# An MLP block in two phases of seven block products: hidden features stored in DRAM, w_out applied by Strassen's scheme

## The chip, the cores and the metric

The kernel runs on one core of one Trainium2 chip. The metric is the device time of one execution in microseconds (us). Engines are named as in the profile: PE does the matmuls, DVE and ACT work elementwise, POOL and SP mostly issue DMAs.

## The reference

One layer of a diffusion transformer, for 2048 tokens of width 1024 with an inner width of 4096, all in fp32:

```python
h = h + gate1 * rmsnorm(short_gated_conv(modulate(rmsnorm(h, g_pre), shift1, scale1)), g_post)
f = square(relu(modulate(rmsnorm(h, g_pre_ff), shift2, scale2) @ w_in)) @ w_out     # 1024 -> 4096 -> 1024
h = h + gate2 * rmsnorm(f, g_post_ff)
```

Shifts, scales and gates come from silu(c) @ ada_w + ada_b. The change is in the second line and in the norm behind it.

## The kernel before

Everything is held transposed: features on the 128 partitions, tokens along the free axis, in NB = 4 token blocks of TB = 512. An fp32 product is made of three fp32r matmuls: each operand is split into a high part (a cast on ACT, L113) and a low part (a subtraction on DVE, L114), and high·high, high·low and low·high are added up in a PSUM bank (`mm3`, `project`, L132). One matmul has a 128x128 weight tile and 512 token columns.

The program has two parts. The conv part runs over the four token blocks and takes about the first third of the span (`conv_in`, `conv_out`); at its end each block's residual stream is stored to DRAM (`hbuf`). The MLP part runs over pairs of token blocks p = (0, 1), (2, 3), and for each pair over NCH = 8 chunks of FC = 512 inner features. In a chunk, `mlp_in` makes the hidden features of both blocks (tile names `hid`, then `r` after the relu, `s` after the square, `hh` as the split pair), and `mlp_out` multiplies them by the chunk's part of w_out (`f`). Each of the 8 x 2 output tiles of a chunk is a PSUM bank of its own that takes 12 matmuls; it is then added by DVE to a running sum in SBUF (`accumulate`, L335; in chunk 0 ACT copies it instead, L333). The six banks of the pool `acc` go round, so a bank that has been filled is not needed again until five others have been filled. Hidden features stay in SBUF.

The last chunk of the last pair is written out by hand (`mlp_last`): the output of the last block is made in two halves of 256 tokens, so that the norm and the residual of the first half (`finish_shared`, shared out over DVE, POOL and ACT) run while PE works on the second half.

The order on each engine is set by a scheduler at build time, which lists every engine's instructions; at run time each engine takes its list in order and waits on semaphores. Weight loads and stores are issued by SP in such an order, too.

Of the kernel before, what the change touches and what calls it, by code (L numbers as in the profile page):

```python
# [9 lines left out]
F32 = mybir.dt.float32  # L10
F32R = mybir.dt.float32r
# [3 lines left out]
P = 128  # L15
# [6 lines left out]
FC = 512  # L22
NCH = DFF // FC
FB = FC // P
EPS = 1e-6


@with_exitstack
def conv_block_kernel(ctx: ExitStack, tc: tile.TileContext, xt, c, cols, ada, w_first, w_sci, w_sco, w_in, w_out,
# [62 lines left out]
    silu = y_pair("silu").rearrange("p s n -> p (s n)")  # L92
# [23 lines left out]
    def load_weights(src, name, n=D, eng=nc.vector):  # L116
        raw = sbuf([P, D], F32, "wraw", 4, f"{name}_raw")
        nc.sync.dma_start(raw[:, :n], src)
        hi = sbuf([P, D], F32R, "whi", 3, f"{name}_hi")
        lo = sbuf([P, D], F32R, "wlo", 3, f"{name}_lo")  # L120
        split(hi[:, :n], lo[:, :n], raw[:, :n], eng)
        return hi, lo
# [17 lines left out]
    class RootMean:  # L140
# [21 lines left out]
        def rows(self):  # L162
            name, n = self.name, self.n
            ps = tp_bank(f"{name}_ps")[:, :n]
            hi, lo = stat_tile(f"{name}_hi", F32R)[:, :n], stat_tile(f"{name}_lo", F32R)[:, :n]
# [11 lines left out]
        def rows_of(self, ps):  # L177
# [6 lines left out]
            r = row_tile(f"{name}_r")[:, :n]  # L184
# [8 lines left out]
    def shifted(v, k, sh, name):  # L193

        hi, lo = act_tile(f"{name}_hi"), act_tile(f"{name}_lo")
# [13 lines left out]
    def mod_tile(j):  # L209

        for m in range(2):
            mod_sum(m, j, sbuf([P, D], F32, "gh", 8, f"ada{j}_{m}"))
# [4 lines left out]
    def mod_rest(m):  # L217

        for j in range(KT):
            mod_sum(m, j, sbuf([P, D], F32, "wraw", 4, f"adar{m}_{j}"))  # L220
            yield
# [14 lines left out]
    def gate_split(q, j):  # L236
        gh, gl = act_tile(f"gh{q}_{j}"), act_tile(f"gl{q}_{j}")
# [3 lines left out]
    def gate(q, j, pc, pv, pb):  # L241
# [29 lines left out]
        if j % 2 == 0:  # L271
            pair = gh_tile(f"g{q}_{j}", F32)
            gated[q, j], gated[q, j + 1] = pair[:, 0], pair[:, 1]
# [14 lines left out]
    def conv_out(q):  # L288
# [11 lines left out]
        for i in range(KT // 2):  # L300
            xr = load_pair(xt[q, i], f"xr{q}_{i}")
# [5 lines left out]
            nc.gpsimd.dma_start(hbuf[q][i], xr)  # L307
        nc.gpsimd.dma_start(rbuf[q], ssh.rows())


    def mlp_in(ch, a, between=None):

        hid = {q: [] for q in a}
        for f in range(FB):
            w = load_weights(w_in[ch * FB + f], f"wi{min(a)}_{ch}_{f}")
            for q in a:
                name = f"{q}_{ch}_{f}"
                ps = acc_bank(f"hid{name}")
                project(w, a[q], ps)
                r = tmp_tile(f"r{name}")  # L320
                nc.scalar.activation(r, ps, AF.Relu)  # L321
                s = tmp_tile(f"s{name}")
                nc.vector.tensor_mul(s, r, r)  # L323
                h = gh_tile(f"hh{name}")
                split(h[:, 0], h[:, 1], s)
                hid[q].append((h[:, 0], h[:, 1]))
            if f == 0 and between:
                between()
        return hid

    def accumulate(y, ps, ch, ss):
        if ch == 0:
            nc.scalar.copy(y, ps)  # L333
        else:
            nc.vector.tensor_add(y, ps, y)  # L335
        if ch == NCH - 1:
            ss.add(y)

    def mlp_out(ch, hid, y, ss):
        for i in range(KT // 2):  # L340
            w = load_weights(w_out[i, ch], f"wf{min(hid)}_{ch}_{i}")
            for s in range(2):
                j = 2 * i + s
                ws = [t[:, s * FC:(s + 1) * FC] for t in w]
                for q in hid:
                    ps = acc_bank(f"f{q}_{ch}_{j}")
                    project(ws, hid[q], ps)
                    accumulate(y[q][j], ps, ch, ss[q])

    def mlp_finish(q, y, r):  # L350
        for i in range(KT // 2):
            hr = load_pair(hbuf[q][i], f"hr{q}_{i}")
            for s in range(2):
# [214 lines left out]
```

## Time and profile before

| what | value |
|---|---|
| median of 3 runs | 2150.74 us (2150.71 to 2150.82) |
| the profiled execution | 2149.79 us, its span 2148.0 us |
| PE busy | 2117.8 us, 99% of the span, 9366 matmuls |
| DVE, ACT, POOL busy | 52%, 31%, 3% |
| DMA | 226.47 MB, mean 105 GB/s |

The profiled execution's own time is 1.79 us above its span. Busy shares are of the span. A matmul's listed length contains the overlap with its neighbours; what one costs in a stream is read from the chain of waits, where a run of matmuls has its start, length and count.

### The profile page before, as it was taken

The numbers are of one execution on the slowest core, as the hardware profiler recorded it, in microseconds if no ns is written. First come the engines' busy times: TensorE is split into PE (matmuls) and PEld (weight loads), VectorE is DVE, ScalarE is ACT, GpSimd is POOL, SyncE is SP. The second block draws the span as 40 slices with busy tenths as digits, with TensorE's granted clock in tenths as the row PEclk, the third lists the DMA queues.
The fourth block names the chain that finished last, engine by engine and source line by source line (L and its number), as shares of the span: only waits on it lengthen the run. The fifth ranks groups of instructions, "written<-read, shape, count | busy, mean of one in ns | idle before, by whom it ended". The sixth has DMA issues, their size and how long they took to land.

```text
span 2148.0 us, 23105 instructions
## 1 busy us (share of the span) xinstructions
PE 2117.8 (99%) x9366; PEld 1749.1 (81%) x9366; DVE 1113.8 (52%) x1626; ACT 655.8 (31%) x940; POOL 69.2 (3%) x72
## 2 busy tenths in 40 slices
PE   7999999999999999999999999999999999999997
PEld 4788888888888888888888888888888888888886
DVE  8877766664655862333333333496233333333356
ACT  3342244433325543121121221353212112121152
POOL 2000000000000000000000000000000000000006
PEclk8999999999999999999999999999999999999998
DMA  8665533432533441111111111136111111111113
GB/s 323 227 225 205 177 138 141 168 134 92 200 139 128 181 172 48 45 46 49 49 49 49 50 49 49 63 124 235 49 49 45 46 49 49 49 49 50 49 59 118
DMA packets 65514, 226.47 MB, mean 105 GB/s; under 512 B 7424, under 2 KB 9472, under 8 KB 65408
## 3 DMA queue, kind: packets, MB, share of 16 engines
q1 hardware_dynamic: 61056, 210.84, 27.9%
q0 software_dynamic: 3776, 13.63, 1.7%
q8 instruction: 73, 1.20, 0.2%
q10 hardware_dynamic: 576, 0.52, 0.1%
q14 instruction: 33, 0.27, 0.0%
HBM read 207.15 MB, written 17.83 MB: 105 GB/s over the span
## 4 chain that ended last, share of the span: by engine, by line
PE 96%; DVE 3%; ACT 0%; issue 0%; DMA 0%; SPq 0%; DVEq 0%
PE hid L132 32%; PE f L132 32%; PE c L132 23%; PE y_ps L132 8%; DVE ada L207 1%; PE c L475 0%; DVE rf_sq L160 0%; DVE a_lo L197 0%; DMA xt<-in_xt_dram 0%; DVE mods L215 0%; DVE a_v L191 0%; DVE f L372 0%; DVE f L335 0%; DVE hr L375 0%; DVE rx_sq L157 0%
## 5 line engine op out<-in xcount | busy, mean ns | idle before, releaser
L132 PE MATMUL f<-hh,wf_hi 128*128 128x512 f32 x1920 | 589.1, 389 | 0.0
L132 PEld LDWEIGHTS f<-hh,wf_hi 128*128 128x128 f32 x1920 | 360.5, 188 | 74.7
L132 PE MATMUL hid<-m_hi,wi_hi 128*128 128x512 f32 x1024 | 398.4, 389 | 0.0
L132 PE MATMUL hid<-m_lo,wi_hi 128*128 128x512 f32 x1024 | 398.4, 389 | 0.0
L132 PE MATMUL hid<-m_hi,wi_lo 128*128 128x512 f32 x1024 | 398.2, 389 | 0.0
L132 PE MATMUL f<-hh,wf_lo 128*128 128x512 f32 x960 | 371.2, 389 | 0.0
L335 DVE TENSOR_TENSOR f<-f,f 128x512 f32<-128x512 f32 (+1 forms) x232 | 155.0, 672 | 313.4 <-PE f L132 313.0
L132 PE MATMUL c<-a_lo,wc_hi 128*128 128x512 f32 x720 | 280.2, 389 | 0.0
L132 PE MATMUL c<-a_hi,wc_hi 128*128 128x512 f32 x720 | 280.1, 389 | 0.0
L132 PE MATMUL c<-a_hi,wc_lo 128*128 128x512 f32 x720 | 279.8, 389 | 0.0
L132 PEld LDWEIGHTS hid<-m_lo,wi_hi 128*128 128x128 f32 x1024 | 192.3, 188 | 39.9
L132 PEld LDWEIGHTS hid<-m_hi,wi_lo 128*128 128x128 f32 x1024 | 192.3, 188 | 39.9
L132 PEld LDWEIGHTS hid<-m_hi,wi_hi 128*128 128x128 f32 x1024 | 192.3, 188 | 39.9
L113 ACT CAST wi_hi<-wi_raw 128x1024 fp32r<-128x1024 f32 x76 | 80.1, 1054 | 442.1 <-PE f L132 369.8
L132 PEld LDWEIGHTS f<-hh,wf_lo 128*128 128x128 f32 x960 | 180.3, 188 | 37.4
L323 DVE TENSOR_TENSOR s<-r 128x512 f32<-128x512 f32 x128 | 89.3, 698 | 143.1 <-ACT r L321 143.1
L132 PEld LDWEIGHTS c<-a_lo,wc_hi 128*128 128x128 f32 x720 | 135.2, 188 | 28.3
L132 PEld LDWEIGHTS c<-a_hi,wc_lo 128*128 128x128 f32 x720 | 135.2, 188 | 28.2
L132 PEld LDWEIGHTS c<-a_hi,wc_hi 128*128 128x128 f32 x720 | 135.2, 188 | 27.8
L113 ACT CAST wc_hi<-wc_raw 128x1024 fp32r<-128x1024 f32 x90 | 94.7, 1053 | 201.2 <-PE c L132 94.5
L114 DVE TENSOR_TENSOR wi_lo<-wi_raw,wi_hi 128x1024 fp32r<-128x1024 f32 x76 | 93.0, 1224 | 117.5 <-ACT wi_hi L113 117.5
L114 DVE TENSOR_TENSOR wf_lo<-wf_raw,wf_hi 128x1024 fp32r<-128x1024 f32 x60 | 73.4, 1224 | 152.9 <-ACT wf_hi L113 152.9
(151 smaller groups left out, 2016.1 us busy)
## 6 DMA issues: line engine op xcount, KB each, us to landing
wc_raw<-in_w_sci_dram SPq DMA_DIRECT2D x90, 512.0 KB, 3.6
wi_raw<-in_w_in_dram SPq DMA_DIRECT2D x76, 512.0 KB, 3.5
wf_raw<-in_w_out_dram SPq DMA_DIRECT2D x60, 512.0 KB, 3.5
adar<-in_ada_dram SPq DMA_DIRECT2D x32, 512.0 KB, 3.7
wo_raw<-in_w_sco_dram SPq DMA_DIRECT2D x32, 512.0 KB, 3.5
xt<-in_xt_dram SPq DMA_DIRECT2D x16, 512.0 KB, 6.4
ada<-in_ada_dram SPq DMA_DIRECT2D x16, 512.0 KB, 8.7
xr<-in_xt_dram SPq DMA_DIRECT2D x16, 512.0 KB, 4.3
```

The source lines that it names most:

```text
L113: nc.scalar.copy(dst_hi, src)
L114: eng.tensor_sub(dst_lo, src, dst_hi.bitcast(F32))
L132: nc.tensor.matmul(ps, l, r, start=first and i == 0, stop=last and i == 2)
L207: nc.vector.scalar_tensor_tensor(t, t, 1.0, silu, op0=ALU.mult, op1=ALU.mult, accum_out=mods[:, m, j:j + 1])
L323: nc.vector.tensor_mul(s, r, r)
L335: nc.vector.tensor_add(y, ps, y)
```

## The change

The MLP part is rearranged. There are now two superblocks s of two token blocks each, and four chunks of 1024 inner features. Seen as a product of 2x2 blocks (output features in two halves, inner features in two halves, the two token blocks as the two columns), each chunk's product with w_out is made from seven block products in place of eight (Strassen's, in Winograd's form). For that, sums and differences of the four hidden blocks (T1 to T4) and of the four weight blocks (S1 to S4) are formed in fp32 on DVE, before the split into high and low parts.

For a superblock, all 16 units `hidden(s, ch, kp)` run first. A unit makes four hidden tiles, their combinations (`features`), seven tiles of 512 KB of split features, and SP stores these in DRAM (`h_store`). Then 16 units `product(...)` run, one for each chunk ch and pair of output tiles jp. Before a chunk its 28 tiles are loaded again through POOL's queue (`load_hidden`); a chunk's weight blocks are combined and split by the generator `weights`. A unit has seven products of 12 matmuls each, in three PSUM banks: bank a takes the products 0, 2, 4 and 6, bank b 1 and 5, bank c 3. After products 0, 2 and 4 the bank's running content is read out into one output block and the next product is added on top, since Winograd's form reuses the sums; after each product DVE adds the bank to an output tile (L461; in chunk 0 some are copied by ACT, L459). The pools of SBUF tiles are merged into three: `ts` of 41, `wf` of 4 and `wr` of 7 tiles of 512 KB. The norm at the end of a superblock works on tiles of both blocks; for s = 0 it is spread over the hidden units of s = 1, for s = 1 it stands at the program's end, on DVE.

```diff
+PRODUCTS = (("a", "11", "11"), ("b", "S1", "T1"), ("a", "S2", "T2"), ("c", "12", "21"), ("a", "S3", "T3"),
+            ("b", "S4", "22"), ("a", "22", "T4"))
+TARGETS = ((0, 0, True), (1, 1, True), (0, 1, True), (0, 0, False), (1, 1, False), (0, 1, False), (1, 0, True))
+    bufs = {"ts": 41, "wf": 4, "wr": 7}
-    def mlp_in(ch, a, between=None):
...
-    def mlp_out(ch, hid, y, ss):
...
-    def mlp_last(ch, a, y):
...
+    def features(y, name, to):
+        y0, y2, y3 = y
+        y1 = pair(f"{name}_y1")
+        nc.vector.tensor_sub(y1[:, 0], y0[:, 1], y0[:, 0])
+        nc.vector.tensor_sub(y2[:, 1], y3[:, 0], y0[:, 1])
+        nc.vector.tensor_sub(y1[:, 1], y3[:, 0], y1[:, 0])
+        nc.vector.tensor_sub(y3[:, 1], y2[:, 0], y1[:, 1])
+        t = pair(f"{name}_11", "ts", F32R)
+        split(t[:, 0], t[:, 1], y0[:, 0])
+        tiles = [t]
+        for i, x in enumerate((y1, y2, y3)):
+            tiles += halves(x, f"{name}_{i}", "ts")
+        for i, t in enumerate(tiles):
+            nc.sync.dma_start(to[i], t.bitcast(F32))
+    def load_hidden(s, ch):
+        tiles = [[None] * 7 for _ in range(KP)]
+        for group in ((0,), (1, 2), (3, 4), (5, 6)):
+            for kp in range(KP):
+                for i in group:
+                    t = tiles[kp][i] = pair(f"h{kp}_{i}", "ts", F32R)
+                    nc.gpsimd.dma_start(t, h_store[s][ch][kp][i].bitcast(F32R))
...
+    def product(a, b, e, name, add, between):
+        banks = {}
+        for m, ((bank, an, bn), (i, j, first)) in enumerate(zip(PRODUCTS, TARGETS)):
+            new = bank not in banks
+            if new:
+                banks[bank] = psum.tile([P, TB], F32, tag="acc", bufs=6, name=f"{name}_{bank}")
+            ps = banks[bank]
+            for kp in range(KP):
+                cs = slice(kp * P, (kp + 1) * P)
+                (lh, ll), (rh, rl) = a[an], b[kp][bn]
+                for n, (l, r) in enumerate(((lh, rh), (lh, rl), (ll, rh))):
+                    nc.tensor.matmul(ps, l[:, cs], r, start=new and kp == 0 and n == 0,
+                                     stop=kp == KP - 1 and n == 2, skip_group_check=True)
+            dst = e[1 + j][:, 0] if i and len(e) == 3 else e[i][:, j]
+            with tc.high_priority():
+                if first and not add:
+                    nc.scalar.copy(dst, ps)
+                else:
+                    nc.vector.tensor_add(dst, ps, dst)
+            between(m)
+    def finish(s, f, ss):
+        r = ss.rows()
+        for k in range(KT):
+            h = load(h_buf[s][k], f"hr{s}_{k}")
+            t = f[k] if s else load(f_buf[k], f"fr{k}")
+            nc.vector.scalar_tensor_tensor(t, t, G5[:, k:k + 1], r, op0=ALU.mult, op1=ALU.mult)
+            nc.vector.tensor_add(h, t, h)
+            nc.sync.dma_start(out[s, k], h)
+            yield
```

Three places show how the instructions stand now. On PE before, where the products with w_out begin in chunk 3 of the first pair (`hid` are hidden banks, `f0_3_0` is block 0, chunk 3, output tile 0):

```order
L132 MATMUL hid1_3_3_7721<-m1_7_hi_5127,wi0_3_3_lo_7686 128x512
L132 MATMUL f0_3_0_7759<-hh0_3_0_7508,wf0_3_0_hi_7755 128x512 x2
L132 MATMUL f0_3_0_7759<-hh0_3_0_7508,wf0_3_0_lo_7756 128x512
...
L132 MATMUL f1_3_0_7773<-hh1_3_0_7540,wf0_3_0_hi_7755 128x512 x2
L132 MATMUL f1_3_0_7773<-hh1_3_0_7540,wf0_3_0_lo_7756 128x512
```

And on PE now, where superblock 0 goes over from its hidden units to its product units (`f0_0_0_a` is superblock 0, chunk 0, unit 0, bank a):

```order
L153 MATMUL hid0_3_3_1_1_8200<-m0_7_hi_5159,wi0_3_3_1_lo_8116 128x512
L454 MATMUL f0_0_0_a_8348<-h0_0_8284,wf0_0_0_11_8260 128x512 x3
L454 MATMUL f0_0_0_a_8348<-h1_0_8286,wf0_0_0_11_8260 128x512 x3
L454 MATMUL f0_0_0_a_8348<-h2_0_8288,wf0_0_0_11_8260 128x512 x3
L454 MATMUL f0_0_0_a_8348<-h3_0_8290,wf0_0_0_11_8260 128x512 x3
L454 MATMUL f0_0_0_b_8362<-h0_1_8292,wf0_0_0_s12_hi_8266 128x512
L454 MATMUL f0_0_0_a_8348<-h0_1_8292,wf0_0_0_s12_hi_8266 128x512
L454 MATMUL f0_0_0_b_8362<-h0_2_8294,wf0_0_0_s12_hi_8266 128x512
```

Before, the next group went into another bank; now bank a takes its second product (with `s12_hi`) one matmul after the 12 of its first, woven with bank b's.

ACT's list now at the same place (`e` are hidden tiles, `h0_3_3_*` the split features of the last hidden unit, `wf0_0_*` weights of product units, L381 the relu, L383 the square, L459 the copy out of a bank):

```order
L136 CAST wf0_0_0_s34_hi_8276<-wf0_0_0_xs_8263 128x1024
L381 ACTIVATE e0_3_3_2_8121<-hid0_3_3_1_1_8200 128x512
L136 CAST h0_3_3_11_8234<-e0_3_3_0_8119 128x512
L383 ACTIVATE e0_3_3_2_8121<-e0_3_3_2_8121 128x512
L136 CAST h0_3_3_0_hi_8237<-h0_3_3_y1_8229 128x1024
L136 CAST h0_3_3_1_hi_8241<-e0_3_3_1_8120 128x1024
L136 CAST h0_3_3_2_hi_8245<-e0_3_3_2_8121 128x1024
L136 CAST wf0_0_1_11_8376<-wf0_0_1_x0_8280 128x512
L459 COPY f0_0_8340<-f0_0_0_a_8348 128x512
```

The copy out of bank a (the last row) stands behind the whole of the last hidden unit's features.

DVE's list at the program's end, before (`f_*` and `hr_*` are the last block's tiles, L372 the scaling, L375 the residual; POOL has a like list beside it):

```order
L335 TENSOR_TENSOR f_3_10366<-f_7_7_256_14906,f_3_10366 128x256
L160 TENSOR_TENSOR rf_1_sq<-rf_1_sq 128x256
L182 SCALAR_TENSOR_TENSOR rf_1_v<-rf_1_ps,rf_1_c 128x256
L183 TENSOR_TENSOR rf_1_v<-rf_1_v,rf_1_c 128x256
L185 SCALAR_TENSOR_TENSOR rf_1_r<-rf_1_v,rf_1_c 128x256
L372 SCALAR_TENSOR_TENSOR f_0_10363<-f_0_10363,mods,rf_1_r 128x256 x2
L375 TENSOR_TENSOR hr_0_14626<-f_0_10363,hr_0_14626 128x256
```

And now (L502 the scaling, L503 the residual, both blocks in one tile; "..." stands for the like rows of tiles 1 to 6):

```order
L461 TENSOR_TENSOR f1_7_13016<-f1_3_3_a_14968,f1_7_13016 128x512 x2
L480 TENSOR_TENSOR rf1_sq_14719<-rf1_sq_14719,rf1_sq_15065 128x1024
L137 TENSOR_TENSOR rf1_lo_15071<-rf1_sq_14719,rf1_hi_15070 128x1024
L490 SCALAR_TENSOR_TENSOR rf1_v_15069<-rf1_ps0_15074,rf1_r_15068 128x512
L490 SCALAR_TENSOR_TENSOR rf1_v_15069<-rf1_ps1_15081,rf1_r_15068 128x512
L491 TENSOR_TENSOR rf1_v_15069<-rf1_v_15069,rf1_r_15068 128x512 x2
L492 SCALAR_TENSOR_TENSOR rf1_r_15068<-rf1_v_15069,rf1_r_15068 128x512 x2
L502 SCALAR_TENSOR_TENSOR f1_0_13009<-f1_0_13009,mods_109,rf1_r_15068 128x1024
...
L502 SCALAR_TENSOR_TENSOR f1_7_13016<-f1_7_13016,mods_109,rf1_r_15068 128x1024
L503 TENSOR_TENSOR hr1_0_15088<-f1_0_13009,hr1_0_15088 128x1024
...
L503 TENSOR_TENSOR hr1_7_15123<-f1_7_13016,hr1_7_15123 128x1024
```

All eight scalings stand ahead of the eight residuals, and none of it is on POOL or ACT.

## Rows read from the trace of the kernel before

**Rows 1.** The page: busy time by engine, and the chain by line.

```profile
PE 2117.8 (99%) x9366; PEld 1749.1 (81%) x9366; DVE 1113.8 (52%) x1626; ACT 655.8 (31%) x940; POOL 69.2 (3%) x72
...
PE hid L132 32%; PE f L132 32%; PE c L132 23%; PE y_ps L132 8%; DVE ada L207 1%; PE c L475 0%; DVE rf_sq L160 0%; DVE a_lo L197 0%; DMA xt<-in_xt_dram 0%; DVE mods L215 0%; DVE a_v L191 0%; DVE f L372 0%; DVE f L335 0%; DVE hr L375 0%; DVE rx_sq L157 0%
```

**Rows 2.** The chain of waits, MLP part: start, length, engine, tile, line, count.

```profile
1300.68 43.52 PE f L132 x192
1344.20 43.52 PE hid L132 x192
...
2107.29 5.77 PE f L132 x48
```

**Rows 3.** Waits of PE: in total, times, longest.

```profile
PE c L475 <- ACT a_hi L196: 7.6, 3, 6.2
PE rf_ps L173 <- DVE rf_sq L160: 3.6, 1, 3.6
PE c L475 <- DVE a_lo L197: 3.2, 3, 2.0
```

**Rows 4.** Groups by line and shape: matmuls f and what DVE adds from them.

```profile
L132 PE MATMUL f<-hh,wf_hi 128*128 128x512 f32 x1920 | 589.1, 389 | 0.0
L132 PE MATMUL f<-hh,wf_lo 128*128 128x512 f32 x960 | 371.2, 389 | 0.0
L335 DVE TENSOR_TENSOR f<-f,f 128x512 f32<-128x512 f32 x216 | 148.8, 691 | 311.6 <-PE f L132 311.2
...
L132 PE MATMUL f<-hh,wl_hi 128*128 128x256 f32 x128 | 23.3, 284 | 0.0
L132 PE MATMUL f<-hh,wl_hi 128*128 128x512 f32 x64 | 19.7, 389 | 0.0
...
L132 PE MATMUL f<-hh,wl_lo 128*128 128x256 f32 x64 | 17.9, 283 | 0.0
L132 PE MATMUL f<-hh,wl_lo 128*128 128x512 f32 x32 | 12.4, 389 | 0.0
```

**Rows 5.** Groups by line and shape: elementwise operations (mean ns behind the busy us).

```profile
L114 DVE TENSOR_TENSOR wf_lo<-wf_raw,wf_hi 128x1024 fp32r<-128x1024 f32 x60 | 73.4, 1224 | 152.9 <-ACT wf_hi L113 152.9
L113 ACT CAST hh<-s 128x512 fp32r<-128x512 f32 x128 | 79.5, 621 | 128.1 <-DVE s L323 128.1
L321 ACT ACTIVATE r<-hid 128x512 f32<-128x512 f32 x128 | 75.8, 592 | 156.6 <-PE hid L132 156.6
L113 ACT CAST wf_hi<-wf_raw 128x1024 fp32r<-128x1024 f32 x60 | 63.3, 1054 | 224.5 <-PE hid L132 132.7 <-PE f L132 87.7 <-issue 3.9
L207 DVE SCALAR_TENSOR_TENSOR adar<-adar,silu 128x1024 f32<-128x1024 f32 x32 | 39.1, 1223 | 40.7 <-DMA adar<-in_ada_dram 40.7
```

**Rows 6.** The timeline around the end of one f group: the last matmul, the addition.

```profile
1303.01 0.39 PE L132 MATMUL f<-hh,wf_lo 128*128 128x512 f32 x1
...
1303.43 0.69 DVE L335 TENSOR_TENSOR f<-f,f 128x512 f32<-128x512 f32 x1
```

**Rows 7.** Windows: busy us (count) of PE, PEld, DVE, ACT, POOL; PEclk, DMA share, GB/s.

```profile
30.00:40.00 10.00, 9.54 (x41) 7.45 (x41) 10.00 (x17) 3.16 (x5) 2.69 (x2) 1.00 1.03 404
1300.00:1340.00 40.00, 40.00 (x178) 33.11 (x178) 15.84 (x20) 5.33 (x6) 0.00 (x0) 1.00 0.15 53
```

**Rows 8.** The page: DMA queues (packets, MB, share of 16 engines' span), and landings.

```profile
q1 hardware_dynamic: 61056, 210.84, 27.9%
...
wf_raw<-in_w_out_dram SPq DMA_DIRECT2D x60, 512.0 KB, 3.5
h<-xr POOLq DMA_DIRECT2D x16, 512.0 KB, 4.8
```

**Rows 9.** Windows of 1 us around an idle stretch of PE, columns as above.

```profile
49.00:50.00 1.00, 0.68 (x3) 0.60 (x4) 1.00 (x3) 1.00 (x3) 0.00 (x0) 1.00 0.72 188
...
56.00:57.00 1.00, 0.00 (x0) 0.00 (x0) 1.00 (x4) 0.00 (x0) 0.00 (x0) 1.00 0.06 25
57.00:58.00 1.00, 0.93 (x3) 0.76 (x4) 1.00 (x3) 0.00 (x0) 0.00 (x0) 0.67 0.00 0
58.00:59.00 1.00, 1.00 (x4) 0.81 (x3) 0.93 (x4) 0.00 (x0) 0.00 (x0) 0.50 0.00 0
59.00:60.00 1.00, 1.00 (x3) 0.73 (x3) 0.90 (x3) 0.70 (x2) 0.00 (x0) 0.50 0.00 0
60.00:61.00 1.00, 1.00 (x4) 0.84 (x3) 1.00 (x2) 1.00 (x3) 0.00 (x0) 0.62 0.67 156
```

**Rows 10.** The timeline of PE: the two idle stretches beside them.

```profile
49.32 1.66 PE L475 MATMUL c<-a_hi,w_hi 128*128 128x512 f32 x6 [1.03 <-ACT a_hi L196]
...
57.07 2.72 PE L475 MATMUL c<-a_lo,w_hi 128*128 128x512 f32 x6 [2.01 <-DVE a_lo L197]
```

**Rows 11.** The timeline at the program's end: PE's last f matmul, the norm, DVE's last.

```profile
2130.89 0.28 PE L132 MATMUL f<-hh,wl_lo 128*128 128x256 f32 x1
...
2135.98 0.38 ACT L181 ACTIVATE rf_c<-rf_ps 128x256 f32<-128x256 f32 x1 [0.77 <-PE rf_ps L174]
...
2144.20 0.42 DVE L375 TENSOR_TENSOR hr<-f,hr 128x256 f32<-128x256 f32 x1
```

More of the change, by code (lines that the diff above doesn't have):

```diff
@@ new lines, in hidden @@
+    def hidden(s, ch, kp, m):
+        name = f"{s}_{ch}_{kp}"
+        w = []
+        for h in range(2):
+            raw = load(w_in[ch, kp, :, 2 * h:2 * h + 2], f"wi{name}_{h}", "wf")
+            w.append(halves(raw, f"wi{name}_{h}", "wr"))
+        e = [pair(f"e{name}_{i}") for i in range(3)]
+        for i in range(2):
+            for q in range(2):
+                ps = acc_bank(f"hid{name}_{i}_{q}")
+                for k in range(KT):
+                    cs = slice(k % KP * P, (k % KP + 1) * P)
+                    mm3(ps, tuple(t[:, i, cs] for t in w[k // KP]), tuple(t[:, q] for t in m[k]), k == 0, k == KT - 1)
+                nc.scalar.activation(e[0][:, q] if i == 0 else e[1 + q][:, 0], ps, AF.Relu)
+        for t in (e[0], e[1][:, 0], e[2][:, 0]):
+            nc.scalar.activation(t, t, AF.Square)
+        features(e, f"h{name}", h_store[s][ch][kp])
@@ new lines, in one, with two @@
+    def one(res, name, t):
+        res[name] = t[:, 0], t[:, 1]
+    def two(res, names, tiles):
+        for i, n in enumerate(names):
+            res[n] = tuple(t[:, i] for t in tiles)
+    def load_hidden(s, ch):
[5 more added lines that the diff above has]
+                    nc.gpsimd.dma_start(t, h_store[s][ch][kp][i].bitcast(F32R))
+        sets = []
+        for x in tiles:
+            res = {}
+            one(res, "11", x[0])
+            for i, names in enumerate((("T1", "T2"), ("21", "T3"), ("22", "T4"))):
+                two(res, names, x[1 + 2 * i:3 + 2 * i])
+            sets.append(res)
+        return sets
@@ L493, in conv_block_kernel @@
                 gate_split(q, j)
-            a2 = {p: a2_of(p, lambda name: gh_tile(name, F32)) for p in range(2)}
+            later["m"] = m_of(0)
         for _ in background:
@@ new lines, in conv_block_kernel, with fetch @@
+    rest = iter(())
+    for s in range(NS):
+        for ch in range(NCH):
+            for kp in range(KP):
+                if s and (ch, kp) == (0, 2):
+                    rest = finish(0, f, ss)
+                hidden(s, ch, kp, later["m"])
+                if (ch, kp) > (1, 0):
+                    next(rest, None)
+        for _ in rest:
+            pass
+        units = [(ch, jp) for ch in range(NCH) for jp in range(KP)]
+        ws = [{} for _ in units]
+        makers = [weights(w_out[jp, ch], f"wf{s}_{ch}_{jp}", w) for (ch, jp), w in zip(units, ws)] + [iter(())] * 2
+        for _ in range(5):
+            next(makers[0])
+        next(makers[1])
+        later["h"] = load_hidden(s, 0)
+        f, ss = [pair(f"f{s}_{j}") for j in range(KT)], PairRootMean(f"rf{s}")
+        def fetch():
+            if ch < NCH - 1:
+                later["h"] = load_hidden(s, ch + 1)
+            elif s < NS - 1:
+                later["m"] = m_of(s + 1)
+        for i, (ch, jp) in enumerate(units):
+            h = later["h"]
+            js = jp, jp + KP
+            e = [f[j] for j in js]
+            product(ws[i], h, e, f"f{s}_{ch}_{jp}", ch > 0, run_makers(makers, i, fetch if jp == KP - 1 else None))
+            if ch == NCH - 1:
+                for j in js:
+                    ss.add(f[j])
+                    if s == 0:
+                        nc.sync.dma_start(f_buf[j], f[j])
@@ L521 @@
+    for _ in finish(NS - 1, f, ss):
+        pass
 _INS = ["xt", "c", "cols", "ada", "w_first", "w_sci", "w_sco", "w_in", "w_out"]
```

306 lines of the change are left out of this document (135 added, 171 removed).

## The prediction

> **What bounds the kernel now.** The page first: PE is busy for 99% of the span, and PE's own lines make up the chain that ended last, hid 32%, f 32%, c 23%, y_ps 8% [rows 1]. Then PE's waits: of any size there are those of c from L475, the first products of the conv part, and 3.6 us for the sums rf_ps in the tail [rows 3]; none is of hid or f. So a matmul saved is time saved at its price in a stream, and every wait that the change brings to PE is time lost. That price comes from the chain, where the matmuls stand back to back: 43.52 us for 192 is 0.2267 us each, and for the 256-column halves 5.77/48 = 0.120 us [rows 2] (a matmul's listed 0.389 us overlaps the next one's).
>
> **The gain.** The w_out product now has 1920 + 960 + 64 + 32 = 2976 matmuls of 512 columns and 128 + 64 = 192 halves [rows 4]: 2976 x 0.2267 + 192 x 0.120 = 697.7 us. After the change there are 2 x 16 units of 7 x 12 = 84: 2688 x 0.2267 = 609.3 us. The gain is **88.4 us**. The hidden product keeps its 3072 matmuls, the conv part its own; there I take 0 (its lists move by a few rows).
>
> **What must stay hidden, and does in the steady part.** A hidden unit lasts 96 x 0.2267 = 21.8 us on PE. By the durations of [rows 4, 5] it needs on DVE 4 differences of 512 (0.69), one low part of 512, three of 1024 (1.22) and two weight splits: 4 x 0.69 + 0.69 + 5 x 1.22 = 9.6 us; on ACT four relus (0.59), squares (about 2.3 in all), casts (0.62 + 5 x 1.05): 10.5 us. A product unit lasts 84 x 0.2267 = 19.0 us: DVE has four weight sums, one low part of 512 and three of 1024, and seven additions out of PSUM, 12 x 0.69 + 3 x 1.22 = 11.9 us; ACT 3.8 us. DMA: the queues ran at 404 GB/s where all 16 engines were busy (share 1.03) [rows 7], so 0.524 MB take 1.30 us; a hidden unit moves 9 such tiles (11.7 us), a product unit 2 tiles of weights and 7 of hidden features, the same. All of it fits, so I charge the steady units nothing. If the cover were gone on DVE, a product unit would have 11.9 us of work to be paid in the place of waits.
>
> The reuse of a bank is the tightest wait in a unit. From the last matmul's start the addition begins 0.42 us later and takes 0.69 [rows 6], so with the way back the bank is free after about 1.17 us. Where 12 matmuls of another bank lie between, PE brings 2.72 us: DVE may be one 1.22-us operation late. That too is 0.
>
> **Where cover is missing.** Five places, each from the lists shown with the change.
>
> *Hidden to product, twice.* Bank a's second product waits for ACT's copy, the last of the nine rows of ACT's list. After the last hidden matmul ACT has: cast 1.05, relu 0.59, cast 0.62, square about 0.6; then DVE needs two differences (1.4) before the cast of y1; then 3 x 1.05, the 0.62 of the lone weight, the copy 0.59: about 9.0 us. PE brings 13 matmuls, 2.95 us. Stall 6.0 us. The clock: after 1.03 us without work PE went on at 1.00, after 2.01 us the granted clock was 0.67, 0.50, 0.50, 0.62 in the next four windows (of the levels 2.4 and 1.2 GHz the lower) [rows 9, 10]; that is 1.7 us of full speed lost. I add 1.6. Then DMA: between the last but one hidden unit's stores and the first product unit's end some 42 tiles (14 stores, 21 loads, weights) want to pass, 42 x 1.30 = 55 us, while PE's way there has about 41 + 6 + 2 = 49 us. Stores and loads take turns, so some loads are late: between 0 (the stores behind the last load may wait) and, at the mean rate of SP's queue while it moved something, 210.84 MB/(0.279 x 2148 us) = 352 GB/s or 1.49 us a tile [rows 8], 63 - 49 = 14 us. The window at full load is the nearer row; I take 3. Together 2 x (6.0 + 1.6 + 3) = **21 us**, bounds 10 and 45.
>
> The Trainium skill (DMA: Bandwidth & Descriptors, Specifications) puts a core's share of HBM at about 358 GB/s, below what the window here shows; by it a tile would take 1.46 us, 42 of them 61.5 us, and these two places would cost about 19 us more, an estimate.
>
> *Chunk to chunk in the product phase, six times.* 28 tiles are loaded; 5 find a free slot early, 23 wait until PE has used the old ones in the chunk's last unit. 23 x 1.30 = 30 us from the first release, where two product units of the new chunk are woven into one another so that the loads are used as late as can be, over 38 us. At 1.30 or 1.49 us a tile I find 8 or 6 us of slack; it is gone at about 1.9 us a tile (276 GB/s). What is left are two short chains a chunk (a weight's cast and low part a few matmuls ahead of their use): 0.5 us each time, **3 us**, bounds 0 and 25.
>
> *Superblock to superblock, once.* The second set of modulated tiles is made as scaling 1.22, ACT about 1.1, low part 1.22, about 3.7 us per tile, against 18 matmuls, 4.1 us; the first two come late, and SP's loads of hm stand behind a weight load that waits for DVE. Before, this place went without a wait of PE [rows 3]. **4 us**, bounds 1 and 8.
>
> *The last unit.* Its last 12 matmuls go into the bank that was filled just before: 1.17 us, and DVE has a 1024 addition (1.22) ahead. **2 us**, bounds 1 and 4.
>
> *The tail.* Before, from the last f matmul (2131.2) to the end of the span (2148.0) 16.8 us [rows 11]. Now, in order: start of the addition and the addition 1.1, square 1.1, addition 1.2, cast 1.05, low part 1.2, four short matmuls 0.8, the root 0.65, six operations of 0.69 (4.1); then eight scalings of 1024 (1.22, as the operation with two tensors and a scalar in [rows 5]) and, all behind them, eight additions of 1.22: 19.6; and the last store. The last DVE operation was followed by 3.4 us before [rows 11], with a store of 128 KB; one of 512 KB lands in 3.5 us or more [rows 8], so 5. Sum 35.8 us, **19 us more** than before, bounds 15 and 22.
>
> **Sum**, against the profiled execution's 2149.8: - 88.4 + 21 + 3 + 4 + 2 + 19 = 2110.4 us. The median of the runs shown is 0.95 us above that execution: **2111 us**. With each bound: 2110 - 11 - 3 - 3 - 1 - 4 = 2088, and 2110 + 24 + 22 + 4 + 2 + 3 = 2165.
>
> **The rivals.** (1) *The gaps close by themselves* (chance 0.12): loads come at 404 GB/s or better, the clock stays up, ACT has caught up. Then only the tail and the 6 us remain: 2150.7 - 88.4 + 19 + 12 = about 2093 us. The early windows speak for the rate; ACT's list speaks against it.
>
> (2) *The load back sets the pace* (0.14). Nearest row for 1.49 us a tile is the queue's mean, and POOL's queue has so far landed 512 KB only in 4.8 us against SP's 3.5 [rows 8]. With 14 us in the two transitions 2111 + 22 = 2133; with 1.9 us a tile also some 4 us in each of six chunk changes, about 2160.
>
> (3) *The bank reuse decides, and the kernel is slower* (0.10). In 32 units x 3 reuses of bank a, 96 places, the addition stands on DVE among weight work that itself waits for PE to free a `wr` tile (7 tiles are one unit's). If it comes 0.4 us late beyond its 2.7 us on average, 39 us are lost and nothing is left; at 0.8 us, 77 us: 2188. For it speaks that DVE took its f additions when they came with 311 us of idle time ahead [rows 4], that is, with nothing in the way, and now has 62% of its time filled; against it the 1.5 us of room in each place. The Trainium skill (TensorE: Matmul & The Clock Gate, A second HAM failure mode) tells of a kernel in which PE's short idle times while going round PSUM banks made the clock swing; here 1.03 us of idle time did not lower it [rows 10], and no row shows many short ones. By that rule rival 3 would come dearer: a half clock for a tenth of the 609 us would be 61 us more, an estimate.
>
> (4) That the change doesn't do what it says, fewer matmuls, is out: the lists have 2688. That the conv part pays for the merged pools I give 0.03 at a few us; it is inside the range.
>
> **How the numbers follow.** My forecast (transitions and tail as priced, 2098 to 2125) has 0.61, rival 1 0.12, rival 2 0.14, rival 3 0.10, other 0.03. The range 2090 to 2152 leaves out the lower part of rival 1 (0.05), the dearest of rival 2 (0.04) and rival 3. Repeats of this kernel lie within 0.01% of each other; 0.2%, 4.3 us, is what I call a change. Faster 0.87 (forecast, rival 1, nearly all of rival 2), same 0.03, slower 0.10.
>
> **What the profile after would show.** Right: some 8870 matmuls; the chain with hid and f of L153 and L454 in runs of many; ACT's copy L459 waited for by PE about 6 us twice; a dip of PEclk behind both; DVE alone for some 20 us at the end. Wrong: PE idle before L454 in every unit, released by DVE L461 (rival 3) or by POOL's loads L400 (rival 2); PE without a wait between hidden and product units (rival 1); a tail under 30 us. A loss of several us in the conv part would break the assumption that it is untouched.

## The result, and the profile after

| | before | changed | 
|---|---|---|
| median of the executions compared | 2150.76 us | 2181.03 us |
| the profiled execution, its span | 2148.0 us | 2177.7 us |
| matmuls, PE busy | 9366, 99% | 8880, 94% |

The changed kernel takes 1.0139 times as long (95% interval 1.0119 to 1.0159): 30 us slower, where 40 us faster was forecast. Its three undisturbed executions took 2179.44 to 2181.25 us; a fourth, of 4111.5 us, is left out of the table and of the ratio.

Where the time went is read by cutting both traces at the starts of three matmuls: the last of y_ps (the conv part's last product), the first of hid after it, the last of f:

| part | before, us | changed, us | difference |
|---|---|---|---|
| conv part, to the last y_ps | 733.1 | 794.2 | +61.1 |
| MLP, first hid to last f | 1397.6 | 1347.8 | -49.8 |
| tail, last f to the end of the span | 17.1 | 35.4 | +18.3 |

So the MLP did gain, and the part that the prediction left out lost more than all of it. The page shows it too: the granted clock (a digit for 1/40 of the span, 54 us) is down in the first slice and in the 14th, which is 708 to 762 us, and PE is at 6 and 7 tenths in the first two.

```profile
PE 2057.7 (94%) x8880; PEld 1683.0 (77%) x8880; DVE 1257.4 (58%) x1691; ACT 784.1 (36%) x1026; POOL 158.2 (7%) x272
...
PE   6799999999999789999998999998999999999993
...
PEclk7999999999999899999999999999999999999997
...
PE hid L153 29%; PE c L153 20%; PE f_a L454 14%; PE y_ps L153 8%; PE f_b L454 7%; PE f_c L454 3%; DMA hs<-h_lo 1%; PE c L552 1%; DMA ada<-in_ada_dram 1%; DMA adar<-in_ada_dram 1%; DMA hm<-hb 1%; DMA h<-hs 1%; POOL h L400 1%; DMA xr<-in_xt_dram 1%; DVE ada L230 0%
```

The waits of PE in the changed kernel (in total, times, longest), where before there were only the first products c and the last norm [rows 3]:

```profile
PE c L552 <- ACT a_parts L219: 30.0, 7, 10.6
PE y_ps L153 <- ACT y L320: 17.2, 2, 16.0
PE f_a L454 <- ACT f L459: 10.7, 2, 5.4
PE hid L153 <- ACT m_hi L343: 7.8, 4, 3.0
PE rh_ps L189 <- ACT rh_parts L136: 7.7, 2, 6.7
...
PE f_b L454 <- DMA h<-hs: 1.1, 2, 0.5
```

Of the first five, three belong to the conv part: 30.0 us at the first products, 17.2 and 7.7 around the y products. The third and fourth are the prediction's own places, hidden to product and superblock to superblock. The chain of waits says what stood behind the conv part's (start, length, engine and what; SPq is SP issuing a DMA, L141 a weight's load, L229 one of ada, L78 the other loads):

```profile
14.27 2.26 POOL w_lo L137
16.55 0.33 SPq L141
16.93 0.42 SPq L229
17.41 6.16 DMA ada<-in_ada_dram
...
710.59 1.05 ACT wo_hi L136
711.64 0.29 SPq L141
...
712.05 3.96 DMA hm<-hb
...
724.86 1.15 ACT m_hi L343
726.01 0.48 ACT y L320
...
726.53 18.69 PE y_ps L153 x73
...
767.27 1.06 ACT wi_hi L136
768.34 0.33 SPq L78
...
768.71 7.02 DMA xr<-in_xt_dram
```

Each time the chain runs through a DMA that SP issues late. At the start SP has the load of a weight (L141) ahead of ada (L229); that weight needs a wf buffer which POOL's w_lo frees at 16.5 us, and so ada's first load goes out at 16.93 us; the chain has the same three steps again at 38, 57 and 76 us. At 712 us it is hm behind a weight wo, and ACT's copy of y, for which PE waits, stands behind three m_hi made from hm. At 768 us it is xr behind a weight wi. SP's lists show the same (the names are shortened, the number at the end tells tiles apart): before,

```
L206 DMA ada_0_157<-in_ada_dram 128x1024
L206 DMA ada_1_160<-in_ada_dram 128x1024
L118 DMA w_0_raw<-in_w_first_dram 128x768
L206 DMA ada_0_195<-in_ada_dram 128x1024
```

and in the changed kernel, at the same place behind the first loads:

```
L141 DMA w_0_raw<-in_w_first_dram 128x768
...
L141 DMA w_4_raw<-in_w_first_dram 128x768
L141 DMA w_5_raw<-in_w_first_dram 128x768
L229 DMA ada_0_382<-in_ada_dram 128x1024
L229 DMA ada_1_385<-in_ada_dram 128x1024
```

The code of that place is the same in both but for the tags from which its tiles come: for ada, gh with 8 slots before, the merged ts now. There are slots enough: in the order of the code, the first ada tile is the 14th of ts's 41. **Theory A:** within a tag the slots are handed out in the order of the code, so the load that opens a tile is put behind the first writers of all tiles that come earlier in the code, statistics and rows among them; loads meant to run ahead no longer do. **Rival B:** the new MLP's modulated tiles, made as wide steps while the conv part ends, load ACT and DVE. **Rival C:** the start is slow because the transfers are.

The windows (busy us and count of PE, PEld, DVE, ACT and POOL; PEclk, DMA share, GB/s) put sizes to the stretches of the changed kernel:

```profile
24.00:92.00 68.00, 45.97 (x147) 34.97 (x148) 47.38 (x72) 13.77 (x18) 11.26 (x5) 0.80 0.50 179
...
722.00:798.00 76.00, 63.59 (x260) 51.40 (x261) 46.20 (x58) 35.95 (x57) 4.89 (x9) 0.88 0.38 125
...
1472.00:1516.00 44.00, 37.25 (x143) 29.39 (x142) 24.25 (x22) 17.43 (x21) 0.00 (x0) 0.88 0.29 111
...
1150.00:1155.00 5.00, 0.00 (x0) 0.00 (x0) 4.58 (x7) 3.66 (x5) 2.70 (x5) 0.87 1.11 414
1155.00:1162.00 7.00, 6.67 (x19) 5.28 (x20) 1.51 (x2) 0.28 (x1) 1.63 (x3) 0.60 1.08 408
1162.00:1170.00 8.00, 8.00 (x37) 6.64 (x36) 2.52 (x3) 3.55 (x5) 1.30 (x3) 1.00 1.08 405
```

The last three are the first stall from hidden to product and what came behind it: PE goes on at the lower of the two clock levels (19 matmuls in 7 us; a stream has 31), then at the full one. DMA moves 405 to 414 GB/s all along, the rate that the prediction took for its tiles [rows 7]. That stall, and the tail, in the timeline:

```profile
1149.59 0.39 PE L454 MATMUL f_b<-h,wf_s_hi 128*128 128x512 f32 x1
1151.34 1.04 ACT L136 CAST h_hi<-h_y 128x1024 fp32r<-128x1024 f32 x1 [1.91 <-DVE h_y L357]
1152.29 1.99 ACT L136 CAST h_hi<-e 128x1024 fp32r<-128x1024 f32 x2
...
1154.70 0.57 ACT L459 COPY f<-f_a 128x512 f32<-128x512 f32 x1
...
1155.33 0.80 PE L454 MATMUL f_a<-h,wf_s_hi 128*128 128x512 f32 x1 [5.36 <-ACT f L459]
...
2142.24 0.39 PE L454 MATMUL f_a<-h,wf_a_lo 128*128 128x512 f32 x1
...
2153.35 9.66 DVE L502 SCALAR_TENSOR_TENSOR f<-f,mods,rf_r 128x1024 f32<-128x1024 f32 x8
2162.93 9.16 DVE L503 TENSOR_TENSOR hr<-f,hr 128x1024 f32<-128x1024 f32 x8
```

ACT's copy is the ninth row of its list there, as the prediction read it, and PE waits 5.36 us for it.

### The profile page after: what moved, and what is told of

It is laid out like the page before. It is cut to its first block, busy times and chain, and to the rows that moved or that the text cites. A ratio compares the mean times of both kernels' runs of the same rounds, so it can differ in the third digit from the quotient of the medians.

```text
span 2177.7 us, 23307 instructions
## 1 busy us (share of the span) xinstructions
PE 2057.7 (94%) x8880; PEld 1683.0 (77%) x8880; DVE 1257.4 (58%) x1691; ACT 784.1 (36%) x1026; POOL 158.2 (7%) x272
## 4 chain that ended last, share of the span: by engine, by line
PE 83%; DMA 6%; DVE 4%; issue 3%; ACT 1%; POOL 1%; SPq 0%; DVEq 0%; POOLq 0%; ACTq 0%
PE hid L153 29%; PE c L153 20%; PE f_a L454 14%; PE y_ps L153 8%; PE f_b L454 7%; PE f_c L454 3%; DMA hs<-h_lo 1%; PE c L552 1%; DMA ada<-in_ada_dram 1%; DMA adar<-in_ada_dram 1%; DMA hm<-hb 1%; DMA h<-hs 1%; POOL h L400 1%; DMA xr<-in_xt_dram 1%; DVE ada L230 0%
## 5 line engine op out<-in xcount | busy, mean ns | idle before, releaser
L153 PE MATMUL c<-a_parts,wc_hi 128*128 128x512 f32 x1440 | 444.6, 390 | 0.7 <-ACT a_parts L219 0.7
L153 PEld LDWEIGHTS c<-a_parts,wc_hi 128*128 128x128 f32 x1440 | 271.1, 188 | 57.7 <-ACT a_parts L219 1.1
L153 PE MATMUL c<-a_parts,wc_lo 128*128 128x512 f32 x720 | 280.7, 390 | 3.4 <-DVE wc_lo L137 3.4
L400 POOL DMA_DIRECT2D h<-hs x224 | 121.2, 541 | 1119.9 <-DMA hs<-h_lo 411.6
L153 PE MATMUL y_ps<-gs,wo_hi 128*128 128x512 f32 x512 | 160.4, 395 | 17.2 <-ACT y L320 17.2
L454 PE MATMUL f_a<-h,wf_s_hi 128*128 128x512 f32 x512 | 163.4, 394 | 10.7 <-ACT f L459 10.7
L454 PE MATMUL f_b<-h,wf_s_hi 128*128 128x512 f32 x512 | 166.8, 394 | 1.4 <-DMA h<-hs 1.1
L153 PEld LDWEIGHTS c<-a_parts,wc_lo 128*128 128x128 f32 x720 | 135.5, 188 | 31.9 <-DVE wc_lo L137 3.9
L137 DVE TENSOR_TENSOR wc_lo<-wc_raw,wc_hi 128x1024 fp32r<-128x1024 f32 x90 | 109.9, 1222 | 82.0 <-PE c L153 47.8
L381 ACT ACTIVATE e<-hid 128x512 f32<-128x512 f32 x128 | 75.2, 596 | 227.4 <-PE hid L153 227.4
L153 PEld LDWEIGHTS y_ps<-gs,wo_hi 128*128 128x128 f32 x512 | 97.6, 191 | 38.6 <-ACT y L320 18.2
```

The source lines that it names most:

```text
L137: eng.tensor_sub(dst_lo, src, dst_hi.bitcast(F32))
L153: nc.tensor.matmul(ps, l, r, start=first and i == 0, stop=last and i == 2)
L381: nc.scalar.activation(e[0][:, q] if i == 0 else e[1 + q][:, 0], ps, AF.Relu)
L400: nc.gpsimd.dma_start(t, h_store[s][ch][kp][i].bitcast(F32R))
L454: nc.tensor.matmul(ps, l[:, cs], r, start=new and kp == 0 and n == 0, stop=kp == KP - 1 and n == 2, skip_group_check=True)
```

## The experiments

All are set against the kernel before, on the same chip; the intervals are 95%. The last three columns are the cuts of above, in us, from one profiled execution of each kernel, whose time lies within 2.8 us of its median.

| kernel | median, us | ratio | to last y_ps | first hid to last f | tail |
|---|---|---|---|---|---|
| e1_pools | 2236.3 | 1.0401 (1.0385 to 1.0416) | 793.7 | 1420.2 | 19.3 |
| e2_ada | 2168.7 | 1.0085 (1.0070 to 1.0100) | 782.1 | 1348.2 | 35.4 |
| e3_end | 2153.9 | 1.0019 (1.0009 to 1.0028) | 768.4 | 1344.7 | 35.4 |
| e4_all | 2138.6 | 0.9948 (0.9934 to 0.9963) | 757.6 | 1343.7 | 35.5 |
| e5_conv | 2121.4 | 0.9866 (0.9850 to 0.9883) | 744.3 | 1340.2 | 35.3 |
| e6_mlp | 2111.6 | 0.9819 (0.9804 to 0.9834) | 744.8 | 1325.3 | 36.9 |
| e7_onemore | 2262.9 | 1.0528 (1.0512 to 1.0543) | 798.2 | 1426.8 | 35.4 |
| e8_adatag | 2169.5 | 1.0088 (1.0073 to 1.0103) | 773.9 | 1358.9 | 34.9 |
| e9_xtag | 2123.5 | 0.9875 (0.9861 to 0.9890) | 739.3 | 1348.2 | 34.9 |
| e10_best | 2106.8 | 0.9804 (0.9784 to 0.9824) | 743.2 | 1326.4 | 34.0 |
| e11_xbest | 2108.6 | 0.9806 (0.9790 to 0.9823) | 739.3 | 1334.5 | 33.9 |

**e1_pools: the kernel before, with the merged tags alone.**

```diff
+    bufs = {"ts": 41, "wf": 4, "wr": 7}
...
-        return sbuf([P, TB], dtype, "st", 5, name)
+        return half("stat", name, dtype)
-        return sbuf([P, 2, TB], F32, "x", 4, name)
+        return pair(name)
-            mod_sum(m, j, sbuf([P, D], F32, "gh", 8, f"ada{j}_{m}"))
+            mod_sum(m, j, flat(pair(f"ada{j}_{m}")))
```

> The kernel before with one part of the change alone: all its tiles from the merged tags (41 pairs ts, 4 wf, 7 wr); its MLP, its product and its order in the code are untouched. Theory A (the merged tag hands out its slots in the order of the code, so loads meant to run ahead stand behind tiles that are computed late): the conv part loses what it lost in the changed kernel, 61 us, almost all of it at the first products (about 25) and around the y products at its end (about 35); so 2195 to 2220 us, ada loads issued at about 17 us into the span instead of 4. Rival B (the conv part lost because of what the new MLP brings into it, the modulated tiles of a superblock made there as eight wide steps): the conv part stays as before, 2150 us +- 5.

The conv part ends 60.6 us later than before; the changed kernel's ended 61.1 us later. The waits of PE are the changed kernel's too:

```profile
PE c L490 <- ACT a_hi L211: 31.4, 7, 10.6
PE y_ps L147 <- ACT y L311: 16.1, 2, 15.0
PE f L147 <- DVE hh L131: 9.9, 2, 5.5
PE rh_ps L182 <- ACT rh_hi L130: 4.6, 1, 4.6
```

So the whole loss of the conv part comes with the merged tags, and B, which has none of it without the new MLP, falls. The time was 16 us above what A expected, because the old MLP lost too (22.6 us; 9.9 of it in the third row, where its second pair of blocks begins).

**e2_ada, e3_end, e4_all: the changed kernel with loads earlier in the code.** e2 has ada's 16 loads and the first four of w0 ahead of the first norm, e3 those of xr and hm earlier, e4 both.

```diff
+    for j in range(KT):
+        for m in range(2):
+            ada_t[j, m] = flat(pair(f"ada{j}_{m}"))
+            nc.sync.dma_start(ada_t[j, m], ada[m, j])
+        if j < 4:
+            raw_t[j] = load_raw(w_first[j], f"w0_{j}", 6 * P)
     ps, ss = tp_bank("rx0_ps"), RootMean("rx0")
...
         g = [parts.pop((q, k)) for k in range(KT)]
+        x = [load(xt[q, i], f"xr{q}_{i}") for i in range(KT // 2)]
...
+            loads = m_loads(0)
             for j in range(KT):
                 gate_split(q, j)
-            later["m"] = m_of(0)
+            later["m"] = m_of(0, loads)
```

> The changed kernel, with the loads of ada and of the first four w0 put ahead of the first root mean in the code; nothing else. Theory A: the issue of ada's loads moves from 17 us to some 4 us into the span, the first block of c products ends some 25 us earlier (at 66 to 70 us instead of 91.5): 2150 to 2160 us. Rival C (the transfers themselves are slower in the merged layout, 205 GB/s against 297 over the start, so that issue order hardly matters): the block's end moves by under 5 us, 2176 to 2181 us.

> The changed kernel, with the loads of xr put at the head of conv_out and the loads of hm ahead of the last gates in the code; nothing else. Theory A: the waits of PE at the conv part's end go (16.4 + 7.0 + 2.0 + 1.5 + 1.7 us of idle time and half of 17 + 10 us at half clock, some 40 us): 2140 to 2153 us. Rival B (these gaps come from ACT's and DVE's extra work for the modulated tiles, not from when the loads are issued): 2170 to 2181 us, with y_ps still waiting for ACT's copy of y.

> The changed kernel with both sets of loads put earlier in the code. Theory A: both gains add, 25 + 35 to 40 us: 2115 to 2125 us, the time that was predicted for the change, and the conv part ends within 5 us of where it ended before (733 us). Rivals B and C: 2165 to 2181 us.

e2 gained 12 us, half of what A expected: the first block's last product starts at 76.4 us (91.1 changed, 65.4 before). DVE now ran seven of ada's multiplications, 8.0 us, in one go ahead of the first a_parts (the 14 of e5's expectation counts each one's reading of the accumulator too); that this block is what was still missing is tried only together with other edits, in e5. C falls: issued early, the same transfers run at 393 to 423 GB/s from 5 to 36 us (in e4) and are then through. e3 gained 27 us of some 40 expected; the wait of y_ps for ACT's y went from 17.2 us to 1.2. Together they made the kernel faster than before, but not by as much as A expected: 24.5 us of the conv part's loss were left.

**e5_conv: the same cure at three more places.** The chain of e4 showed that block on DVE, an xt load issued at 177 us, and hm(1) behind weight loads on SP.

```diff
-        with tc.issue_after(first) if k else ExitStack():
+        with tc.issue_after(behind[k]):
             mod_tile(k)
...
-    r = x_rows(1)
+    r, ts = x_rows(1), xt_loads(1)
...
-            v = vs[k] if vs else load(h_buf[s][k], f"hm{s}_{k}")
+            v = vs[k] if vs else load(h_buf[s][k], f"hm{s}_{k}", eng=nc.gpsimd)
```

> The fourth kernel (loads of ada, xr and hm early in the code, 2138.6 us), and three more places of the same kind: ada's multiplications on DVE held behind the rx sums and woven with the a_parts (14 of them had run in one block at 26.9 us), the loads of xt for a_of put in front of the conv block that hides them, and the second superblock's loads of hm issued by POOL, where no weight load stands ahead of them. Theory A (what is left of the loss is again order: work that is ready early or late in the lists): first block of c ends at 66 to 70 us (75.7 there), no gap of PE at 176 to 199 us (7.2 us there), gaps at the superblock change from 9.6 to under 4 us and no half clock behind them: 2105 to 2118 us. Rival (the merged tags hold too few tiles, so that what is gained in one place is lost in the next): 2130 to 2140 us.

The block's last product starts at 69.7 us, no gap is left at 176 to 199 us (one of 2.0 at 257), and the largest gaps at the superblock change are 1.6 + 3.0 us (a gap here and below is from the start of one matmul to the start of the next). 17 us were gained, 3 less than the least expected.

**e8_adatag, e9_xtag: the code in its order, the loads in a tag of their own.** This parts the order of the code from the tag.

```diff
-    bufs = {"ts": 41, "wf": 4, "wr": 7}
+    bufs = {"ts": 37, "wf": 4, "wr": 7, "x": 4}
...
-            mod_sum(m, j, flat(pair(f"ada{j}_{m}")))
+            mod_sum(m, j, flat(pair(f"ada{j}_{m}", "x")))
...
-            xr = load(xt[q, i], f"xr{q}_{i}")
+            xr = load(xt[q, i], f"xr{q}_{i}", "x")
...
-            v = load(h_buf[s][k], f"hm{s}_{k}")
+            v = load(h_buf[s][k], f"hm{s}_{k}", "x")
```

(This is e9; xs and xt likewise. e8 has only the line of ada, with the tag named ada.)

> The changed kernel with its code in the same order; only ada's 16 tiles come from a tag of their own (4 slots, ts with 37 in place of 41). Theory A (order of the code counts within one tag only): ada's first loads are issued at 4 us into the span again, the first block of c ends at 66 to 72 us in place of 91: 2155 to 2163 us. Rival (code order decides across tags too, so that the earlier kernels gained only because their code was moved): the block's end stays at about 91 us, 2180 us. If the MLP needs the four slots, it loses some us after 794 - 22 = 772 us.

> The same tag of 4 slots for all loads that run ahead in the conv part and for hm (ada, xs, xt, xr, hm); ts 37, code in the same order as in the changed kernel. Theory A: the conv part loses almost nothing any more, its last y product ends at 735 to 747 us (733 before, 794 changed): 2122 to 2135 us. Rival: as for the eighth kernel, or the loss moves to another place because ts is smaller: over 2150 us.

In e8 ada's first load is issued at 3.8 us (first and last issue of the 16 loads are in the row below) and the block's last product starts at 68.4 us, with ts four slots smaller: the tag decides, not room, and not the place in the code across tags.

```profile
L229 SPq DMA_DIRECT2D ada<-in_ada_dram x16: 328/328/597, 3.8 to 49.0; - x16
```

Its time was over 6 us above the expectation because the MLP lost 11 us with 37 slots; PE's waits for h were 6.9 us there against 1.1. e9 is the changed kernel with six lines edited, and its conv part is the kernel before's but for 6.2 us; its windows:

```profile
24.00:66.00 42.00, 37.32 (x143) 27.74 (x142) 40.60 (x61) 12.42 (x16) 12.37 (x6) 0.92 0.83 279
66.00:724.00 658.00, 657.28 (x2897) 543.54 (x2896) 455.16 (x722) 259.21 (x360) 14.24 (x26) 1.00 0.49 166
```

The first block, whose stretch took 68 us in the changed kernel, takes 42, and from 66 to 724 us PE is without work for 0.7 us in all. Its MLP takes the 1348 us of the changed kernel's: what hm in x saves at the superblock change goes in waits for h (7.6 us against 1.1), as ts is smaller. 2123.5 us is what the change is worth when the conv part keeps its order.

**e6_mlp, e10_best, e11_xbest: the prediction's stall and tail.** In the last hidden unit the three wide casts are put behind the copies out of the banks; in the tail scaling and addition are woven. e6 gives three additions to POOL, e10 none; e11 is e9 with e10's edits.

```diff
+            if m < 3 and parts:
+                with tc.issue_after(ins):
+                    next(parts, None)
...
-            nc.vector.scalar_tensor_tensor(t, t, G5[:, k:k + 1], r, op0=ALU.mult, op1=ALU.mult)
-            nc.vector.tensor_add(h, t, h)
+            with tc.issue_after(adds[-2]) if s and len(adds) > 1 else ExitStack():
+                nc.vector.scalar_tensor_tensor(t, t, G5[:, k:k + 1], r, op0=ALU.mult, op1=ALU.mult)
+            if s and k in (0, 2, 4):
+                nc.gpsimd.tensor_add(h, t, h)
+            else:
+                adds.append(nc.vector.tensor_add(h, t, h).ins)
```

> The fifth kernel, with the three wide casts of the last hidden unit's features put behind the first product's copies on ACT (f taken unit by unit so that its slots suffice), and in the tail scaling and addition woven, three of the eight additions on POOL, the last store in two halves. By the prediction's term for hidden to product (PE waits for ACT's copy, the last of nine rows): the gap of 5.74 us at both places falls under 1.5 us and the half clock behind it (6.8 us long) goes, 2 x 8 = 16 us; the tail from 35.5 to about 31 us: 19 to 22 us under the fifth kernel. Rival (the gap has a second releaser close behind, the load back of the last hidden features): the gap stays over 4 us, released by DMA h<-hs, and only the tail is gained, 4 us.

> The sixth kernel (2111.6 us) with all eight additions of the tail on DVE again, still woven with the scalings and with the last store in halves. If POOL's additions held DVE up there (an addition on DVE took 3.35 us beside one on POOL, 1.21 without): tail from 37.0 to 33 to 35 us, 2107 to 2110 us. If not: 2112 us or more.

> The ninth kernel with the sixth's order from hidden to product and the woven tail, all on DVE. If the gap of 5.74 us there is ACT's order alone, 16 us at both places and 1 to 2 in the tail are gained on the ninth kernel, although ts has 37 slots only: 2104 to 2118 us. If the 37 slots are too few for the deferred casts, the first unit waits for h instead, and the gain is under 8 us.

The stall is gone and with it the dip of the clock: in the 76 us around the first one e5 and e6 have

```profile
1094.00:1170.00 76.00, 69.20 (x293) 55.34 (x293) 36.82 (x46) 24.48 (x34) 15.24 (x29) 0.96 0.84 301
```

```profile
1094.00:1170.00 76.00, 73.17 (x317) 58.61 (x316) 40.24 (x50) 26.02 (x36) 14.61 (x27) 1.00 0.81 291
```

24 matmuls more, 5.4 us at 0.2267; over the MLP 14.9 us against e5. The tail got 1.6 us longer in place of 4 shorter (see the last section), so that e6 gained 10 us where 19 to 22 were expected; with all additions on DVE (e10) the tail is 34.0 us. e11 gains 13.7 us of the MLP on e9 and 1 in the tail. e10 and e11 are 2.0% and 1.9% faster than the kernel before.

**e7_onemore: the price of a block product.** The changed kernel, with 12 matmuls more in each unit, into bank c, whose result nothing reads.

```diff
             between(m)
+        for kp in range(KP):
+            cs = slice(kp * P, (kp + 1) * P)
+            (lh, ll), (rh, rl) = a["12"], b[kp]["T4"]
+            for n, (l, r) in enumerate(((lh, rh), (lh, rl), (ll, rh))):
+                nc.tensor.matmul(banks["c"], l[:, cs], r, start=kp == 0 and n == 0,
+                                 stop=kp == KP - 1 and n == 2, skip_group_check=True)
```

> The changed kernel with an eighth block product in each of the 32 units: 12 matmuls more into bank c, whose result nothing reads. By the prediction's price (a matmul in a stream is 0.2267 us of time, nothing else bounds a unit): 32 x 12 x 0.2267 = 87 us more, 2181 + 87 = 2268 (2262 to 2272). Rival (a product unit is partly set by DVE's additions or by the load back, so that PE's matmuls are partly under cover): less, 2181 + 40 to 70 us.

The time was as expected. The MLP took 79.0 us more, 0.206 us for each of the 384 matmuls against 0.2267. The price itself holds: in the changed kernel 20 of the 32 units, from first matmul to first matmul of the next, take 19.04 us, 84 x 0.2267, and here 25 of them 21.76 us, 96 x 0.2267. What is missing to 87.0 us are waits that the added matmuls covered: what the starts of the MLP's matmuls lie further apart than 0.2267 us, summed, is 40.6 us in the changed kernel and 32.6 here.

## Why the prediction was wrong, point by point

**The step that failed** is "the conv part its own; there I take 0 (its lists move by a few rows)", with the 0.03 "at a few us" for the merged pools. It was 61.1 us. Merged tags alone make all of it (e1), and loads in a tag of their own take all but 6.2 us away with the code's order unchanged (e9). The prediction laid PE's, ACT's and DVE's lists beside each other at three places in the MLP; SP's list at the program's start, where a term of 0 rested on prefetches, was not among them; it differs from its row 7 on. The prediction named the sign itself ("A loss of several us in the conv part would break the assumption that it is untouched") but gave it 0.03; its 0.10 for a slower kernel stood on rival 3, which did not come. That the scheduler gives a merged tag's slots in the order of the code is inferred from these lists and kernels; it was not tried with other sizes of the tag.

The terms, beside what the runs showed. In the MLP's rows "measured" is what the starts of the matmuls there lie further apart than 0.2267 us, summed; the gain is the matmuls that are no longer there at that price, which 20 units keep to the hundredth of a us.

| term | predicted, us | measured, us |
|---|---|---|
| conv part | 0 | +61.1 |
| gain of the products | -88.4 | -88.4 |
| hidden to product, twice | 21 | 20.9 |
| six chunk changes | 3 | 1.5 |
| superblock change | 4 | 13.4 |
| last unit | 2 | 1.3 |
| conv part's last rows, in the hidden units | no term | 3.3 |
| tail | 19 | 18.3 |

**Hidden to product.** Mechanism, place and size were right: each place lost 5.5 us to the wait for ACT's copy (6.0 predicted). Behind the two waits the matmuls, most of them at the lower clock, cost 5.7 us together (1.6 each predicted), and the second units lost 4.2 us, 1.1 of it in waits for h of over 0.25 us (3 each predicted for the DMA). That the three parts add up to the 21 is partly luck: the clock came dearer and the DMA cheaper.

**Superblock change.** It was mis-sized, 13.4 us against 4 with an upper bound of 8. The reason was named in the prediction, hm behind a weight load on SP, with the first two tiles late; PE waited at four tiles, which cost 8.4 us, and the matmuls behind these waits, in part at the lower clock (0.88 on average in the window of 1472 to 1516 us), cost another 5.0 us. A full stream has 194 matmuls in that window; it has 143.

**The MLP's sum** without the tail was put at -88.4 + 21 + 3 + 4 + 2 = -58.4 us and was -49.8. The measured terms give -88.4 + 20.9 + 1.5 + 13.4 + 1.3 + 3.3 = -48.0, and the stretch has 8 short matmuls of the norms less than before, 1.8 us. That closes the sum. Of the 8.6 us between forecast and measurement, 9.4 are the superblock change and 3.3 the conv part's last rows, which ran late into the hidden units (gaps of 1.5 and 1.7 us at 829 and 831 us); the smaller terms go the other way.

**The rivals.** None of the three came: the gaps did not close by themselves; the load back did not set the pace, though POOL's loads of h took 9.9 us to land (median); and 20 units run at the full pace of a stream, matmul behind matmul, so the bank's reuse cost nothing there; the one wait of PE for a bank's addition of over 0.25 us is the 1.0 us of the last unit. The Trainium skill (DMA: Bandwidth & Descriptors, Specifications) puts a core's share of HBM at about 358 GB/s; the windows at and behind the stall show 405 to 414 GB/s, and the measurement decides. The case that decided was the fourth, "that the change doesn't do what it says", read too narrowly: the matmuls were counted, what else the diff touched was not.

**The tail** was right in its steps: 35.8 us worked out from the end of the last f matmul against 35.0 measured from there (35.4 from its start), eight scalings and eight additions in 18.8 us.

## What to carry to other kernels

When a change merges pools or tags, the order of the loads is part of the change: lay the list of the engine that issues them beside the old one from the first row on, for parts too whose arithmetic is untouched. Loads that are meant to run ahead want a tag (or a queue) that nothing computed late shares; four slots were worth 55 us of the conv part here. The saving in matmuls was real at its full price, and the waits that it brought were forecast to within about 10 us in all; the loss lay in a part that the change was not meant to touch.

## What the hardware showed that was not expected

Operations on DVE stood still beside an addition on POOL. In e6 DVE's addition of two SBUF tiles took 3.35 us, twice, each time beginning about 1 us behind the start of POOL's and ending about 1.1 us behind its end:

```profile
2087.35 3.26 POOL L523 TENSOR_TENSOR hr<-f,hr 128x1024 f32<-128x1024 f32 x1 [1.21 <-DVE f L521]
2088.34 3.35 DVE L525 TENSOR_TENSOR hr<-f,hr 128x1024 f32<-128x1024 f32 x1
...
2093.02 3.26 POOL L523 TENSOR_TENSOR hr<-f,hr 128x1024 f32<-128x1024 f32 x1 [2.41 <-issue]
2094.01 3.35 DVE L525 TENSOR_TENSOR hr<-f,hr 128x1024 f32<-128x1024 f32 x1
...
2098.48 1.21 DVE L525 TENSOR_TENSOR hr<-f,hr 128x1024 f32<-128x1024 f32 x1
```

The same addition with POOL idle took 1.21 us, the last row. POOL's first addition, at 2082.98, held a scaling instead, which reads two SBUF tiles as well: 3.36 us in place of 1.28. A scaling that was under way when POOL began kept its ordinary time (at 2082.66 and 2087.14). So three additions given to POOL held DVE up by 2.1 us each and saved it 1.2 each, and the tail grew; it is 2.9 us shorter in e10. The kernel before shows it too: at 32.15 us one of ada's multiplications took 2.86 us in place of 1.22, beside a subtraction of POOL's from 31.98 to 33.92. The Trainium skill (GPSIMD Engine Reference, Key points) says that the two engines share their SBUF interfaces and contend when DVE reads two SBUF inputs; these rows agree, and give it a size: DVE's operation ended 1.08 us behind POOL's each time, as if it had done nothing until POOL was nearly through.
